# Three of a pair's four weight sums in DRAM, in two halves, and the fourth on VectorE

## The chip, the cores and the metric

The kernel runs on one core of a Trainium2 chip. The metric is device time in microseconds for one execution of the whole program; the number compared is the median of several runs.

A core has five engines, each with its own instruction stream that it works through in order: TensorE (PE, matrix products), VectorE (DVE), ScalarE (ACT), GpSimd (POOL) and SyncE (SP, here only a queue that starts transfers). They are held together by semaphores. Transfers between DRAM and the on-chip memory are carried out by 16 DMA engines, which all queues share. GpSimd's queue can also start a copy that adds to its target ("accumulating copy").

## The reference, cut to what matters

One decoder layer on 256 tokens of width 1024: pooling and attention heads in parallel, an output projection and a layer norm, a cross-attention into 256 memory tokens and a layer norm, and then the part that this case is about:

```python
def swiglu(h, w_gate, w_up, w_down):
    return (jax.nn.silu(h @ w_gate) * (h @ w_up)) @ w_down

h = layer_norm(DEEPNORM_ALPHA * h + swiglu(h, w_gate[l], w_up[l], w_down[l]), ln3_g[l], ln3_b[l])
```

The inner width is 2816. All inputs and outputs are float32.

## The kernel before

**Two terms per number.** TensorE multiplies a reduced float32 (called F32R) at full speed. So each operand is split into `hi`, its value rounded to F32R, and `lo`, the rest; a product is made of three: hi·hi, hi·lo and lo·hi (`three`, lines 386 to 391). Splitting a weight tile of 128 x 1024 takes one cast on ScalarE (L171) and one subtraction on VectorE (L173).

**The stream of weights.** Class `Stream` holds all weight tiles in the order of use: w0, w1, and so on. `fetch` starts the load of a tile on SP's queue into one of seven raw buffers, `prepare` splits it, and `fetch_ahead` starts as many loads as there are raw buffers that no unsplit tile holds. Split tiles lie in eight pairs of buffers (nine from the third gate/up chunk on). Each engine's order is the order in which the program writes its instructions; no scheduler moves them. A load hook (`ws.before`) puts other transfers into SP's order ahead of a given tile.

**Gate and up.** The inner width is cut into 11 chunks of 256 columns. Chunk c uses four weight tiles; chunk 1 begins with w63 and chunk 10 ends with w102. Its four PSUM banks are read out by ScalarE (L990) and VectorE (L991, four adds of 128 x 256), and these instructions stand in the engines' order behind the splits of the tiles of the following chunk. Two sets of four banks alternate, so that chunk c + 2, or the first products of the last stage, wait until the banks of chunk c are read out. What comes out of a chunk is multiplied, split (L456, L457) and kept as `gT`.

**Down.** The last projection runs over the same 11 chunks. Chunks 1 to 8 are multiplied by a scheme with seven products in place of eight for two-by-two blocks: a chunk's 256 rows and the two halves of the columns make four quarters of weights, each 128 x 512. Besides the quarters the scheme needs sums of them. For chunks 7 and 8 VectorE makes those sums from the loaded quarters (`prepare_pair`, lines 123 to 147; three tiles of numbers for each chunk, w124 to w129). For chunks 1 to 6 (`SUMMED`) the sums are made in DRAM before the tiles are loaded. The host has put the quarters of these chunks in order in `w_sum`, four planes of [128, 6, 512]; the program makes two arrays of [128, 2, 6, 512]:

- `sum_z` begins as a copy of planes 1 and 2, and gets planes 2 and 3 added: (plane 1 + plane 2, plane 2 + plane 3).
- `sum_w` begins as a copy of planes 0 and 1; both its halves get the second sum of `sum_z` added, and its first half plane 1 as well.

The two plain copies of 3 MB each are started by SP (L353, L354), ahead of tiles w62 and w63. The four accumulating copies are in `add_quarters` (L356 to L363, issued by L358) on POOL's queue: one of 3 MB and three of 1.5 MB. POOL reaches them after the second layer norm's last small instruction.

Per chunk the stream then loads tile `y` (planes 0 and 1), `z` and `w`, and for every second chunk `o` (plane 3 of two chunks), each 128 x 1024. In the order of the stream they are y, o, z, w and y, z, w: w103 to w123. `summed` (L1080) multiplies them; each tile takes two products of three, on accumulators m[0] to m[7], which fill the eight banks. Chunks 0, 9 and 10 (w130 to w135) are multiplied plainly by `pieces`, and the layer norm ends the program.

Of the kernel before, what the change touches and what calls it, by code (L numbers as in the profile page):

```python
# [8 lines left out]
F32 = mybir.dt.float32  # L9
F32R = mybir.dt.float32r  # L10
AF = mybir.ActivationFunctionType
OP = mybir.AluOpType
AX = mybir.AxisListType

P = 128
# [24 lines left out]
SUMMED = (1, 2, 3, 4, 5, 6)  # L40
# [6 lines left out]
def r32(t):  # L47
    return t.bitcast(F32)


class Stream:
# [2 lines left out]

    def __init__(self, nc, raw_pool, pool):
        self.nc, self.raw_pool, self.pool = nc, raw_pool, pool
        self.pairs, self.corner = {}, {}
        self.src, self.raws, self.tiles, self.homes = [], [], [], []
        self.loads, self.splits = {}, {}
        self.used, self.held = 0, True  # L60
        self.pace, self.asked = 1, 0
        self.cuts, self.casts = {}, {}
        self.late, self.ahead = None, W_BUFS
# [8 lines left out]
    def add_pair(self, upper, lower):  # L72

        first = len(self.src)
        self.src += [upper, lower, None]
        for i in range(3):
            self.pairs[first + i] = (first, i)
        return range(first, first + 3)  # L80

    def before(self, number, load):

        self.loads.setdefault(number, []).append(load)
# [5 lines left out]
    def fetch(self, upto, queue):  # L90

        while len(self.raws) < min(upto, len(self.src)):
            i = len(self.raws)
            for load in self.loads.pop(i, []):
                load()
            src = self.src[i]
            if i < len(self.homes):
                raw = self.homes[i]
            else:
                raw = self.raw_pool.tile(self.shape(i), F32, tag="raw", name=f"w{i}r")  # L100
            if src is not None:
                for s, q in self.cuts.get(i, [(slice(None), queue)]):
                    q.dma_start(raw[:, :, s], src[:, :, s])
            self.raws.append(raw)

    def shape(self, i):
        return list((self.src[i - 1] if self.src[i] is None else self.src[i]).shape)

    def widen(self, pool):
# [3 lines left out]
    def fetch_ahead(self):  # L113

        while len(self.raws) < len(self.src):
            i, done = len(self.raws), len(self.tiles)
            waiting = [j for j in range(len(self.homes), i)
                       if (self.pairs[j][0] + 2 if j in self.pairs else j) >= done]
            if len(waiting) >= RAW_BUFS:
                break  # L120
            self.fetch(i + 1, self.nc.sync)
# [27 lines left out]
    def prepare(self, upto, eng=None):  # L149
        nc = self.nc  # L150
        while len(self.tiles) < min(upto, len(self.src)):
            i = len(self.tiles)
            src = self.src[i]
            for split in self.splits.pop(i, []):
                split()
            self.fetch(i + 1, nc.sync)
            raw = self.raws[i]
            shape = self.shape(i)
            pool = self.pool
            if self.late and (i - self.late[0]) % self.ahead < LATE_BUFS:  # L160
                pool = self.late[1]
            hi = pool.tile(shape, F32R, tag="hi", name=f"w{i}h")
            lo = pool.tile(shape, F32R, tag="lo", name=f"w{i}l")
            if i in self.pairs:
                self.prepare_pair(i, hi, lo)
                self.tiles.append((hi, lo))
                self.fetch_ahead()
                continue
            for group in self.casts.get(i, [[slice(None)]]):
                for s in group:  # L170
                    nc.scalar.copy(hi[:, :, s], raw[:, :, s])  # L171
                s = slice(group[0].start, group[-1].stop)
                (eng or nc.vector).tensor_sub(lo[:, :, s], raw[:, :, s], r32(hi[:, :, s]))  # L173
            self.tiles.append((hi, lo))
            self.fetch_ahead()
# [32 lines left out]
def decoder_layer(  # L208
# [3 lines left out]
    nc = tc.nc  # L212
# [14 lines left out]
    def bank(name):  # L227
        return pb.tile([P, 512], F32, tag="b", name=name)
# [5 lines left out]
    ws = Stream(nc, rp, wp)  # L234
# [5 lines left out]
    def rows(w, k0, c0, nk=1, width=D):  # L240
        return ws.add(w[k0 * P:(k0 + nk) * P, c0:c0 + width].rearrange("(k p) n -> p k n", p=P), 1)

    def block(w, at, shape):

        j, n = shape
        return w[at:at + P * j * n].rearrange("(p j n) -> p j n", p=P, j=j)

    c_qk = []
    for k in range(KD):
        if k < 3:  # L250
            first = [ws.add(block(w_qkv, (2 * k + j) * P * 512, (1, 512)), 1)[0] for j in range(2)]
# [6 lines left out]
    c_u = [cols(w_u, c) for c in range(2)]  # L258
    c_xk = [cols(w_xk, c) for c in range(4)]
    c_mix = [rows(w_out, k, 0) for k in range(KD)]  # L260
    for numbers in c_mix[:5]:
        ws.cuts[numbers[0]] = [(slice(0, 512), nc.sync), (slice(512, D), nc.sync)]
    c_xv = [rows(w_xkv, k, D) for k in range(KD)]
    c_xq = [cols(w_xq, c) for c in range(4)]
    c_xo = [rows(w_xo, k, 0) for k in range(KD)]
    c_gu = [ws.add(w_gu[c], 4) for c in range(NFC)]
    dram = ctx.enter_context(tc.tile_pool(name="dram", bufs=1, space=bass.MemoryType.DRAM))
    sum_z, sum_w = [dram.tile([P, 2, len(SUMMED), 512], F32, name=f"sum_{name}") for name in "zw"]
    c_dn = {}
    for c in DOWN:  # L270
        tiles = [w_down[k * P:(k + 1) * P, :].rearrange("(k p) n -> p k n", p=P) for k in (2 * c, 2 * c + 1)]
        if c in SUMMED:
            j = SUMMED.index(c)
            order = [("y", w_sum[:, 0:2, j, :]), ("z", sum_z[:, :, j, :]), ("w", sum_w[:, :, j, :])]
            if j % 2 == 0:
                order.insert(1, ("o", w_sum[:, 3, j:j + 2, :]))
            c_dn[c] = {what: ws.add(src, 1)[0] for what, src in order}
        elif c in SEVEN:
            c_dn[c] = ws.add_pair(*tiles)
        else:  # L280
            c_dn[c] = [ws.add(w, 1)[0] for w in tiles]
# [68 lines left out]
    ws.before(c_dn[LAST[0]][1], load_norm("b", 3, ln3_b))  # L350


    ws.before(c_gu[0][3], lambda: nc.sync.dma_start(sum_z, w_sum[:, 1:3]))  # L353
    ws.before(c_gu[1][0], lambda: nc.sync.dma_start(sum_w, w_sum[:, 0:2]))  # L354

    def add_quarters():  # L356
        def add(dst, src):
            nc.gpsimd.dma_start(dst, src, accum_op=OP.add, max_dma_last_dim=8192)  # L358

        add(sum_z, w_sum[:, 2:4])  # L360
        for i in range(2):
            add(sum_w[:, i], sum_z[:, 1])
        add(sum_w[:, 0], w_sum[:, 1])  # L363

    ident = cp.tile([P, P], F32, name="ident")
    make_identity(nc, ident)
# [29 lines left out]
    def proj_both(pss, numbers, yT, group=KD):  # L396

        for k0 in range(0, KD, group):  # L400
            for k in range(k0, k0 + group):
                hi, _ = ws.get(numbers, k)
                for b, ps in enumerate(pss):
                    nc.tensor.matmul(ps, hi[:, b * P:(b + 1) * P], yT.both(k), start=k == 0, stop=False,  # L404
                                     skip_group_check=True)
                yield
            for k in range(k0, k0 + group):
                _, lo = ws.parts_of(numbers, k)
                for b, ps in enumerate(pss):
                    nc.tensor.matmul(ps[:, S:], lo[:, b * P:(b + 1) * P], yT.pair(k)[0], start=False,  # L410
                                     stop=k == KD - 1, skip_group_check=True)
                ws.done(numbers, k)
                if ws.pace == 1:
                    ws.next()
                yield
# [31 lines left out]
    def run(gen, n=None):  # L447

        while n is None or n > 0:
            if next(gen, gen) is gen:  # L450
                return False
            n = None if n is None else n - 1
        return True
# [559 lines left out]
    first = [bank("pg") for t in range(T)]  # L1013
# [10 lines left out]
    for c in range(1, NFC):  # L1024
        pss = [(accbank if c % 2 else bank)("pg") for _ in range(4)]
        if c == 3:
            ws.widen(late)
            add_quarters()
        gu = proj_both(pss, c_gu[c], h2T, KD if c < NFC - 3 else 2)
        run(gu, 2)  # L1030
        if left:
            left.multiply()
        run(gu, 2)
        if left:
            left.split()
        else:
            run(gu, 4)
            gated_t()
        if c == NFC - 1:
            run(gu, 7)  # L1040
            ws.held = True
        run(gu)
        left = Gated(c, pss)
        left.add()
# [200 lines left out]
```

## Time and profile before

| | us |
|---|---|
| median of 3 runs | 378.41 (377.07 to 378.56) |
| profiled execution, whole | 378.57 |
| its span, first to last instruction | 376.8 |
| PE busy in the span | 368.5 |
| DVE busy | 298.2 |
| ACT busy | 206.6 |
| POOL busy | 24.5 |

The profile is one execution, seen by the hardware profiler. The granted TensorE clock was 0.999 of full speed. Of 90.80 MB moved, 82.13 MB went through SP's queue and 7.86 MB through POOL's, which is that of the accumulating copies; the latter took 10.3% of the 16 DMA engines' time.

In a row of the chain stand start, length, engine, tile and line. A row of a timeline has start and length in us, engine, line, operation, output and inputs with their shapes, a count, and in brackets how long the engine stood idle before it and what released it. The length of an instruction on VectorE or ScalarE reaches a little into the next one, so starts are compared where instructions follow each other. In a list of transfers, the last number is the time from issue to landing. In a list of waits stand the total, the count and the longest. The last stage (down) begins at 314.98 us of the span.

### The profile page before, as it was taken

What the parts mean: (1) busy time and instruction counts of PE and PEld (TensorE: products, weight loads), DVE (VectorE), ACT (ScalarE), POOL (GpSimd) and SP (SyncE); (2) the same over time, 40 slices, a digit from 0 to 9 for tenths busy, and PEclk for the clock granted to TensorE, in tenths of its full rate; (3) what the DMA queues carried; (4) which work ended last, traced back from release to release, by engine and by line L of the source; (5) the groups of instructions that cost most, each with busy time, mean ns of one, the idle gap of its engine ahead of it and who ended that gap; (6) DMA issues with size and microseconds to landing.
All of it is one profiled execution on the core that took longest, in us unless ns stands there. A gap on an engine that the chain in (4) does not pass through costs nothing.

```text
span 376.8 us, 5614 instructions
## 1 busy us (share of the span) xinstructions
PE 368.5 (98%) x2058; PEld 317.2 (84%) x2058; DVE 298.2 (79%) x481; ACT 206.6 (55%) x330; POOL 24.5 (6%) x31
## 2 busy tenths in 40 slices
PE   9999999999999999999999999989999999999994
PEld 8997878787888889988888888868888888888882
DVE  6768799965699677865887468688888889989994
ACT  5746677644164636644145446465567668865510
POOL 1000033400010000000120101010000000000021
PEclk9999999999999999999999999999999999999999
DMA  7997674668509965998149999999655668996302
GB/s 268 414 416 270 217 286 139 198 221 285 165 0 301 374 214 181 348 334 315 57 79 232 340 272 355 291 318 335 236 192 172 199 195 255 300 401 260 94 0 111
DMA packets 26715, 90.80 MB, mean 241 GB/s; under 512 B 2624, under 2 KB 3392, under 8 KB 25920
## 3 DMA queue, kind: packets, MB, share of 16 engines
q1 hardware_dynamic: 25040, 82.13, 61.8%
q0 software_dynamic: 1216, 7.86, 10.3%
q10 hardware_dynamic: 432, 0.46, 0.3%
q8 instruction: 16, 0.26, 0.3%
q14 instruction: 11, 0.09, 0.1%
HBM read 89.39 MB, written 15.20 MB: 278 GB/s over the span
## 4 chain that ended last, share of the span: by engine, by line
PE 96%; DVE 1%; DMA 1%; ACT 1%; issue 0%; POOLq 0%; ACTq 0%
PE pg L404 20%; PE pg L410 10%; PE pqk L510 6%; PE m L389 5%; PE m L391 5%; PE m L390 5%; PE acc L389 4%; PE acc L390 4%; PE acc L391 4%; PE pxk L404 4%; PE pxq L404 4%; PE pxq L410 2%; PE pu L404 2%; PE pxk L410 2%; PE xv L389 2%; PE xv L391 2%
## 5 line engine op out<-in xcount | busy, mean ns | idle before, releaser
L456 ACT CAST g<-sg 128x512 fp32r<-128x512 f32 x16 | 9.9, 620 | 20.7 <-DVE sg L1010 14.8
L752 POOL TENSOR_TENSOR rs<-rs,mhalf 128x1 f32<-128x1 f32 x6 | 5.0, 832 | 238.5 <-DVE rs L751 238.5
L457 DVE TENSOR_TENSOR g<-sg,g 128x512 fp32r<-128x512 f32 x16 | 11.1, 692 | 9.6 <-ACT g L456 9.6
L991 DVE TENSOR_TENSOR sg<-pg,sg 128x256 f32<-128x256 f32 x40 | 14.1, 416 | 0.0
L990 ACT COPY sg<-pg 128x256 f32<-128x256 f32 x40 | 11.8, 378 | 0.6 <-PE pg L410 0.6
L995 ACT ACTIVATE sg<-sg 128x512 f32<-128x512 f32 x10 | 6.4, 635 | 10.0 <-DVE sg L991 10.0
L547 ACT ACTIVATE xpr<-xs,mx 128x256 f32<-128x256 f32 x8 | 3.7, 469 | 14.3 <-DVE mx L558 14.3
L547 ACT ACTIVATE pr<-pr,mx 128x128 f32<-128x128 f32 (+1 forms) x16 | 7.1, 445 | 7.6 <-DVE mx L578 7.6
L456 ACT CAST h2T<-tp 128x512 fp32r<-128x512 f32 x4 | 2.3, 586 | 13.0 <-PE tp L467 12.9
L757 DVE SCALAR_TENSOR_TENSOR r<-r,mv,gb 128x512 f32<-128x512 f32 (+2 forms) x12 | 8.2, 722 | 0.0
L744 DVE BATCH_NORM_STATS2 st<-r 128x6 f32<-128x512 f32 (+1 forms) x12 | 8.0, 670 | 0.3
L623 POOL TENSOR_TENSOR win<-upad 128x542 f32<-128x542 f32 x2 | 4.0, 1998 | 57.0 <-DVE upad L654 57.0
L996 DVE TENSOR_TENSOR sg<-sg 128x512 f32<-128x512 f32 x10 | 6.9, 691 | 0.8
L552 DVE RECIPROCAL sm<-sm 128x2 f32<-128x2 f32 x12 | 2.0, 166 | 6.0 <-ACT xpr L547 4.5
L862 PE MATMUL xs<-xkTh,xq 128*128 128x256 f32 x32 | 6.4, 282 | 0.0
L456 ACT CAST h1T<-tp 128x512 fp32r<-128x512 f32 x4 | 2.4, 588 | 7.1 <-PE tp L467 7.1
L762 DVE SCALAR_TENSOR_TENSOR h<-r,rs,gb 128x512 f32<-128x512 f32 x8 | 5.7, 747 | 0.1
L623 POOL TENSOR_TENSOR win<-win 128x269 f32<-128x269 f32 (+3 forms) x4 | 5.8, 1445 | 0.2
L662 ACT CAST xkTh<-pxk 128x256 fp32r<-128x256 f32 x8 | 2.6, 377 | 5.5 <-PE pxk L410 5.5
L664 DVE TENSOR_TENSOR xkl<-pxk,xkTh 128x256 f32<-128x256 f32 x8 | 3.0, 416 | 3.1 <-ACT xkTh L662 3.1
L862 PEld LDWEIGHTS xs<-xkTh,xq 128*128 128x128 f32 x32 | 5.2, 190 | 0.2
L171 ACT CAST w39h<-w39r 128x1024 fp32r<-128x1024 f32 x1 | 1.0, 1049 | 7.8 <-PE acc L391 7.8
(1132 smaller groups left out, 1286.4 us busy)
## 6 DMA issues: line engine op xcount, KB each, us to landing
sum_z<-in_w_sum SPq DMA_DIRECT2D x1, 3072.0 KB, 13.5
sum_w<-in_w_sum SPq DMA_DIRECT2D x1, 3072.0 KB, 18.8
sum_z<-in_w_sum POOLq DMA_DIRECT2D x1, 3072.0 KB, 21.1
sum_w<-sum_z POOLq DMA_DIRECT2D x2, 1536.0 KB, 15.6
gb<-in_ln_g SPq DMA_DIRECT2D x3, 512.0 KB, 6.2
gb<-in_ln_b SPq DMA_DIRECT2D x3, 512.0 KB, 9.2
sum_w<-in_w_sum POOLq DMA_DIRECT2D x1, 1536.0 KB, 14.6
wr<-in_w_qkv SPq DMA_DIRECT2D x5, 256.0 KB, 4.4
```

The source lines that it names most:

```text
L389: nc.tensor.matmul(ps, wa, ya, start=start, stop=False, skip_group_check=part)
L390: nc.tensor.matmul(ps, wa, yb, start=False, stop=False, skip_group_check=part)
L391: nc.tensor.matmul(ps, wb, ya, start=False, stop=stop, skip_group_check=part)
L404: nc.tensor.matmul(ps, hi[:, b * P:(b + 1) * P], yT.both(k), start=k == 0, stop=False, skip_group_check=True)
L410: nc.tensor.matmul(ps[:, S:], lo[:, b * P:(b + 1) * P], yT.pair(k)[0], start=False, stop=k == KD - 1, skip_group_check=True)
L456: nc.scalar.copy(h, ps)
L457: nc.vector.tensor_sub(l, ps, r32(h))
L510: nc.tensor.matmul(qk[i][:, f, :], w[:, c * P:(c + 1) * P], y, start=k == 0 and f == 0 and w is hi and y is x_hi, stop=k == KD - 1 and w i ...
L547: nc.scalar.activation(dst[:, j, :], src[:, j, :], AF.Exp, bias=mx[:, j:j + 1], scale=sign, accum_out=sm[:, j:j + 1])
L862: nc.tensor.matmul(ps[:, t, :], q[:, kk, t * P:(t + 1) * P], k[:, 2 * h + kk], start=n == 0, stop=q is q_lo and kk == 1, skip_group_check= ...
L990: nc.scalar.copy(y[:, f, :], ps[:, S:])
L991: nc.vector.tensor_add(y[:, f, :], ps[:, :S], y[:, f, :])
```

## The change

Tile w is made in two steps. Its second half (the sum of planes 1, 2 and 3) is still made in DRAM: `sum_w` now is [128, 6, 512], a copy of plane 1 to which the second sum of `sum_z` is added. The load brings this half only, 128 x 512, into the second half of the raw tile. The first half is made on chip: VectorE adds the first half of the chunk's raw tile y to it (L183 of the changed kernel), into the first half of the raw tile; then the tile is split like any other. The raw buffer of y is therefore held until that add (`held_raw`).

The order within a chunk becomes y, o, w, z and y, w, z; w is w105, w108, w112, w115, w119 and w122. In VectorE's order the add stands directly ahead of the subtraction of its tile, and ScalarE's cast of the tile reads what the add writes.

The copies in DRAM are made in two halves of three chunks each: on SP's queue 1.5 MB for `sum_z` ahead of w63 and 0.75 MB for `sum_w` ahead of w65, then the same for the second half ahead of w67 and w69. On POOL's queue there are again four accumulating copies: 1.5 MB, 0.75 MB, 1.5 MB, 0.75 MB; each pair's second reads what the first wrote.

Of the eight row blocks of `w_out` (w27 to w34), the first three instead of the first five are loaded in two halves of the columns.

```diff
+    def add_fourth(self, src, of):
+
+        number = len(self.src)
+        self.src.append(src)
+        self.fourth[number] = of
+        self.held_raw[of] = number
+        return number
...
-            if src is not None:
+            if i in self.fourth:
+                queue.dma_start(raw[:, 1:2, :], src)
+            elif src is not None:
...
             waiting = [j for j in range(len(self.homes), i)
-                       if (self.pairs[j][0] + 2 if j in self.pairs else j) >= done]
+                       if self.held_raw.get(j, j) >= done]
...
+            if i in self.fourth:
+                nc.vector.tensor_add(raw[:, 0], self.raws[self.fourth[i]][:, 0], raw[:, 1])
             for group in self.casts.get(i, [[slice(None)]]):
...
-    for numbers in c_mix[:5]:
+    for numbers in c_mix[:3]:
...
-    sum_z, sum_w = [dram.tile([P, 2, len(SUMMED), 512], F32, name=f"sum_{name}") for name in "zw"]
+    sum_z = dram.tile([P, 2, len(SUMMED), 512], F32, name="sum_z")
+    sum_w = dram.tile([P, len(SUMMED), 512], F32, name="sum_w")
...
-            order = [("y", w_sum[:, 0:2, j, :]), ("z", sum_z[:, :, j, :]), ("w", sum_w[:, :, j, :])]
+            c_dn[c] = {"y": ws.add(w_sum[:, 0:2, j, :], 1)[0]}
             if j % 2 == 0:
-                order.insert(1, ("o", w_sum[:, 3, j:j + 2, :]))
-            c_dn[c] = {what: ws.add(src, 1)[0] for what, src in order}
+                c_dn[c]["o"] = ws.add(w_sum[:, 3, j:j + 2, :], 1)[0]
+            c_dn[c]["w"] = ws.add_fourth(sum_w[:, j:j + 1, :], c_dn[c]["y"])
+            c_dn[c]["z"] = ws.add(sum_z[:, :, j, :], 1)[0]
...
-    ws.before(c_gu[0][3], lambda: nc.sync.dma_start(sum_z, w_sum[:, 1:3]))
-    ws.before(c_gu[1][0], lambda: nc.sync.dma_start(sum_w, w_sum[:, 0:2]))
-
-    def add_quarters():
-        def add(dst, src):
-            nc.gpsimd.dma_start(dst, src, accum_op=OP.add, max_dma_last_dim=8192)
-
-        add(sum_z, w_sum[:, 2:4])
-        for i in range(2):
-            add(sum_w[:, i], sum_z[:, 1])
-        add(sum_w[:, 0], w_sum[:, 1])
+    HALF = len(SUMMED) // 2
+
+    def begin_sums(i):
+        js = slice(i * HALF, (i + 1) * HALF)
+        nc.sync.dma_start(sum_z[:, :, js], w_sum[:, 1:3, js])
+
+    def begin_second(i):
+        js = slice(i * HALF, (i + 1) * HALF)
+        nc.sync.dma_start(sum_w[:, js], w_sum[:, 1, js])
+
+    for i in range(2):
+        ws.before(c_gu[i + 1][0], lambda i=i: begin_sums(i))
+        ws.before(c_gu[i + 1][2], lambda i=i: begin_second(i))
+
+    def add_quarters(i):
+        js = slice(i * HALF, (i + 1) * HALF)
+        nc.gpsimd.dma_start(sum_z[:, :, js], w_sum[:, 2:4, js], accum_op=OP.add, max_dma_last_dim=8192)
+        nc.gpsimd.dma_start(sum_w[:, js], sum_z[:, 1, js], accum_op=OP.add, max_dma_last_dim=8192)
...
-            add_quarters()
+            for i in range(2):
+                add_quarters(i)
```

More of the change, by code (lines that the diff above doesn't have):

```diff
@@ L56, in __init__ @@
         self.nc, self.raw_pool, self.pool = nc, raw_pool, pool
-        self.pairs, self.corner = {}, {}
+        self.pairs, self.corner, self.fourth, self.held_raw = {}, {}, {}, {}
         self.src, self.raws, self.tiles, self.homes = [], [], [], []
@@ L79, in add_pair @@
             self.pairs[first + i] = (first, i)
+            self.held_raw[first + i] = first + 2
         return range(first, first + 3)
+    def add_fourth(self, src, of):
[4 more added lines that the diff above has]
+        return number
     def before(self, number, load):
@@ L106, in shape @@
     def shape(self, i):
+        if i in self.fourth:
+            i = self.fourth[i]
         return list((self.src[i - 1] if self.src[i] is None else self.src[i]).shape)
@@ L168, in prepare @@
                 continue
+            if i in self.fourth:
+                nc.vector.tensor_add(raw[:, 0], self.raws[self.fourth[i]][:, 0], raw[:, 1])
             for group in self.casts.get(i, [[slice(None)]]):
```

## The prediction

> **What bounds the kernel now.** I read the page's first part, the chain and PE's waits, then the stretches and each engine's timeline. All rows are of one profiled execution: its span is 376.8 us, its own time 378.57 us, 0.16 us above the median of the three runs (378.41 us), so 1.77 us lie outside the span and are left alone.
>
> ```profile
> PE 368.5 (98%) x2058; PEld 317.2 (84%) x2058; DVE 298.2 (79%) x481; ACT 206.6 (55%) x330; POOL 24.5 (6%) x31
> PE pg L404 <- DVE sg L991: 1.9, 1, 1.9
> 223.50 7.28 PE pg L404 x32
> ...
> 234.61 7.28 PE pg L404 x32
> ...
> 245.89 1.23 DVE w83l L173
> 247.11 0.34 DVE sg L991
> 247.59 7.81 PE pg L404 x32
> ...
> 259.24 7.28 PE pg L404 x32
> ```
>
> TensorE is the bound. Inside the work it stops once: a gate/up chunk takes 234.61 to 247.59 = 12.98 us and the next one 11.65 us, where the undisturbed one from 223.50 took 11.11 us. The hole so costs 1.87 + 0.54 = **2.4 us**. What it waited for stands on VectorE, ScalarE and GpSimd:
>
> ```profile
> 191.51 1.44 POOL L358 DMA_DIRECT2D sum_z<-in_w_sum  x1
> 244.78 1.15 POOL L358 DMA_DIRECT2D sum_w<-in_w_sum  x1 [14.79 <-issue]
> sum_z<-in_w_sum POOLq DMA_DIRECT2D x1, 3072.0 KB, 21.1
> sum_w<-sum_z POOLq DMA_DIRECT2D x2, 1536.0 KB, 15.6
> sum_w<-in_w_sum POOLq DMA_DIRECT2D x1, 1536.0 KB, 14.6
> 243.55 1.05 ACT L171 CAST w82h<-w82r 128x1024 fp32r<-128x1024 f32 x1 [2.26 <-DMA w82r<-in_w_gu]
> 244.64 1.23 DVE L173 TENSOR_TENSOR w82l<-w82r,w82h 128x1024 fp32r<-128x1024 f32 x1 [1.90 <-ACT w82h L171]
> 210.31 1.22 DVE L173 TENSOR_TENSOR w70l<-w70r,w70h 128x1024 fp32r<-128x1024 f32 x1 [5.02 <-ACT w70h L171]
> 219.63 1.23 DVE L173 TENSOR_TENSOR w74l<-w74r,w74h 128x1024 fp32r<-128x1024 f32 x1 [1.57 <-ACT w74h L171]
> 229.61 1.23 DVE L173 TENSOR_TENSOR w76l<-w76r,w76h 128x1024 fp32r<-128x1024 f32 x1 [1.46 <-ACT w76h L171]
> w71r<-in_w_gu SPq DMA_DIRECT2D x1, 512.0 KB, 13.8
> w76r<-in_w_gu SPq DMA_DIRECT2D x1, 512.0 KB, 23.4
> ```
>
> From 191.5 to 259.4 us four accumulating copies run one after another, and weight loads land late beside them. The load of w82 makes VectorE late, and the evacuation of an earlier chunk's banks (L991) stands behind it in VectorE's order. The same starvation costs VectorE 5.02 + 1.57 + 1.46 + 1.90 = 9.95 us by then; it is still catching up at the end of the stage. The last stage (from 314.98) has no such hole, but VectorE is full:
>
> ```profile
> 315.00:330.00 15.00, 15.00 (x67) 12.40 (x67) 15.00 (x18) 12.59 (x17) 0.00 (x0) 1.00 0.89 275
> 314.98 0.23 PE m L389
> 315.51 1.41 DVE L991 TENSOR_TENSOR sg<-pg,sg 128x256 f32<-128x256 f32 x4
> 347.90 1.23 DVE L147 TENSOR_TENSOR w129l<-w127r,w129h 128x1024 fp32r<-128x1024 f32 x1
> 351.79 0.39 PE L390 MATMUL m<-w129l,g 128*128 128x512 f32 x1
> ```
>
> (Columns of a stretch: length, then PE, PEld, DVE, ACT, POOL busy.) VectorE needs all of 15 us, and w129l, done at 349.13, is read at 351.79: the smallest lead of the late tiles, **2.66 us**.
>
> **The change, part by part.**
>
> *Less traffic.* The accumulates shrink from 3 + 1.5 + 1.5 + 1.5 to 1.5 + 0.75 + 1.5 + 0.75 MB, the plain copies from 6 to 4.5 MB. POOL issues four as before, in order, each pair's second waiting for its first; they still start at 191.5. The first takes 10.5 us (half of 21.1) to 15.6; I take 10.5, since like the old one it starts before this stage's loads. The 1.5 MB one later takes 15.6, a 0.75 MB one 7.8 (half) to 15.6 at most; I take half. With 1.15 us an issue they end near 191.5 + 41.7 + 3.5 = 236.7, not 259.4. In one 15.6 us accumulate six tiles landed (w71 to w76, issued at 199.31 and 204.99, landed 13.8 and 23.4 us later), 2.6 us a tile. From w70 near the first one's end, 203, that puts w82 at 203 + 12 x 2.6 = 234, not 243.5. Without VectorE's 1.90 us for w82 alone L991 comes 1.9 us sooner, just what PE waits there; with the earlier waits shrunk too the hole closes with several us to spare. **-2.4 us** (nothing, at the other end).
>
> [...]
>
> *SP's queue.* It gets four copies instead of two, before w63, w65, w67 and w69 instead of w62 and w63.
>
> ```profile
> 179.92 0.33 SPq L103 DMA_DIRECT2D w69r<-in_w_gu  x1
> 195.84 1.05 ACT L171 CAST w63h<-w63r 128x1024 fp32r<-128x1024 f32 x1
> ```
>
> The last copy so goes out near 180, at a quarter of the size of the old ones, and no tile behind a copy is cast before 195.84. Two w_out rows are loaded whole instead of in halves: two issues of 0.33 us fewer, and PE's list of waits names no load. Both at nothing: the cover is the seven raw buffers; without it, a late load costs its lateness.
>
> *The fourth sum.* Six times, for w105, w108, w112, w115, w119 and w122, VectorE adds 128x512, then ScalarE casts, then VectorE subtracts. VectorE's order has nothing between add and subtraction, so it stands still while ScalarE casts. The pairs of the last chunks show that step:
>
> ```profile
> 339.33 0.68 DVE L143 TENSOR_TENSOR w124r<-w125r,w124r 128x512 f32<-128x512 f32 x1
> 339.93 1.22 DVE L144 TENSOR_TENSOR w125l<-w126r,w125h 128x1024 fp32r<-128x1024 f32 x1
> 340.12 1.05 ACT L146 CAST w126h<-w124r 128x1024 fp32r<-128x1024 f32 x1 [1.67 <-DVE w124r L143]
> 341.21 1.23 DVE L147 TENSOR_TENSOR w126l<-w124r,w126h 128x1024 fp32r<-128x1024 f32 x1
> ```
>
> From add to subtraction 341.21 - 339.33 = **1.88 us**; with the wait filled, as there by L144, an add costs 0.60. So 0.60 to 1.88 each; I take 1.88, as nothing fills it here. Behind the waiting subtraction stand all later splits and L991, and PE waits for those.
>
> The first two (w105, w108) lie before the last evacuation, which cannot start before PE is done at 314.98. VectorE reached it at 315.51, with no slack, so they would cost 2 x 1.88 less two small idles, 3.2 us, if VectorE came as now. It comes earlier: of the 9.95 us of starvation 2.4 + 3.2 = 5.6 must vanish for them to be hidden. Loads some 9 us earlier at w82 give that; **0** (3.2 at the other end).
>
> The other four cost 4 x 1.88 = 7.52 us of VectorE. Against that its waits for loads in this stage go, as it becomes slower than the loads:
>
> ```profile
> 329.46 1.22 DVE L173 TENSOR_TENSOR w120l<-w120r,w120h 128x1024 fp32r<-128x1024 f32 x1
> 331.47 1.22 DVE L173 TENSOR_TENSOR w121l<-w121r,w121h 128x1024 fp32r<-128x1024 f32 x1 [0.79 <-ACT w121h L171]
> 334.15 1.23 DVE L173 TENSOR_TENSOR w123l<-w123r,w123h 128x1024 fp32r<-128x1024 f32 x1
> 335.29 0.69 DVE L136 TENSOR_TENSOR w126r<-w124r 128x512 f32<-128x512 f32 x1
> 336.38 0.69 DVE L137 TENSOR_TENSOR w126r<-w125r,w124r 128x512 f32<-128x512 f32 x1 [0.40 <-DMA w125r<-in_w_down]
> 365.37 0.69 DVE L1136 TENSOR_TENSOR r<-m,r 128x512 f32<-128x512 f32 x1 [0.24 <-PE m L391]
> 367.52 0.42 DVE L1136 TENSOR_TENSOR r<-m,r 128x256 f32<-128x256 f32 x1 [0.73 <-PE m L391]
> 369.90 0.43 DVE L744 BATCH_NORM_STATS2 st<-acc 128x6 f32<-128x256 f32 x1 [1.49 <-PE acc L391]
> ```
>
> A split follows a split after 1.14 us. 0.87 us are lost before w121l, 0.40 from there to w123l, 0.49 before L137: 1.76 us. VectorE is 7.52 - 1.76 = 5.76 us late at w129l, the lead is 2.66, so PE is **+3.1 us** late. Behind that VectorE is 2.66 us late against PE, and the tail's idles hold 0.24 + 0.73 + 1.49 = 2.46: **+0.2**.
>
> *Raw buffers and smaller loads.* y's buffer is held until w's add, so one or two of seven loads start later; half-size w loads land sooner. Loads in that stage take 4 to 8 us and seven splits now take over 10: nothing, and a late load would cost VectorE its lateness. TensorE's products are the same 2058 in another order.
>
> Sum: 378.57 - 2.4 + 3.1 + 0.2 = **379.5 us**, +0.2%; against the median 0.16 less, within what I can claim.
>
> **Rivals.**
>
> *The lead isn't won* (20%). The loads come just early enough to close the hole, but the first two sums also stand on VectorE's path: + 3.2, 382.7 us. For it: a first accumulate of 15.6 us and small ones near 15.6 would keep the loads late to about 245. Against it: six tiles landed beside one.
>
> *The hole stays* (8%). Loads late as now, or another one on the edge: 382.7 + 2.4 = 385.1 us.
>
> *VectorE keeps up* (12%), the other side. If the add costs its 0.60 alone, because the casting engine is not waited for, the four cost 2.4 us, less 1.76, well inside 2.66: PE isn't delayed, and 378.57 - 2.4 = 376.2 us. It decides below (2.66 + 1.76) / 4 = 1.1 us a sum. Against it: that order has no other work to fill the wait.
>
> *A slowed TensorE clock* (3%). In the stretch of the hole the granted clock stayed 1.00, though the chunk behind it took 0.54 us too long. If PE's 3.1 us came as one wait and the clock then fell to half for as long, the loss would be 1.7 us more, 381.2 us; I expect waits of at most about 1 us each, spread over w119 to w129. [...]
>
> ```profile
> 244.80:250.00 5.20, 3.32 (x17) 2.52 (x16) 4.39 (x8) 3.39 (x7) 1.14 (x1) 1.00 1.06 369
> ```
>
> **How the numbers follow.** The likeliest case (52%) gives 379.5, its own range 378.5 to 381.0 (0.2 of the hole left, waits 0.1 to 0.3 us longer). 5% stay for what I don't see. Half a per cent, 1.9 us, is about what a measurement tells from no change: 376.5 to 380.3 is the same. The likeliest puts 0.40 there and 0.12 above; the lost lead, the staying hole and the slow clock add 0.31 above; keeping up gives 0.11 below. With the rest: faster 0.11, same 0.45, slower 0.44. From 377.4 to 383.0 the range leaves out the hole that stays and keeping up, 2 in 10.
>
> **What would show it.** PE's wait for L991 is gone and chunks keep 11.1 us; the last accumulate is issued near 228, not 244.78. Add to subtraction is 1.9 us on each of six w tiles. PE gets short waits for splits between w119 and w129, about 3 us. Wrong if loads still land 13 us or more after 230, if L991 of the last chunk starts well behind PE's end, or if PE has no waits in the last stage.

## The result, and the profile after

The changed kernel takes 380.37 us (median of 6 runs, 379.94 to 381.24) against 378.22 us before (6 runs, 377.07 to 378.56): a ratio of 1.0064, 95% interval 1.0047 to 1.0081. It is slower by about 2 us; 379.5 was forecast, with a range of 377.4 to 383.0.

The profiled execution took 380.30 us, with a span of 378.5 us and a granted clock of 0.999; the one of before 378.57 and 376.8. The rows below are to be compared with the rows of before in the prediction. First the page's busy times and PE's list of waits (total, count, longest) of the changed kernel:

```profile
PE 370.2 (98%) x2058; PEld 317.5 (84%) x2058; DVE 301.2 (80%) x487; ACT 206.2 (54%) x330; POOL 23.5 (6%) x31
PE m L414 <- DVE w127l L153: 0.8, 1, 0.8
PE m L414 <- DVE w124l L153: 0.8, 1, 0.8
PE m L414 <- DVE w127c L151: 0.2, 1, 0.2
```

The 1.9 us wait for the evacuation of the banks is gone. In its place stand waits for splits of the last chunks' tiles, and none of a whole microsecond. The chain of the changed kernel shows the gate/up chunks at an even pace:

```profile
235.13 7.28 PE pg L428 x32
...
246.25 7.28 PE pg L428 x32
...
257.36 7.28 PE pg L428 x32
```

Each takes 11.1 us, the one that took 12.98 before and its successor (11.65) too. The hole is closed: 2.4 us won. The accumulating copies are shorter and the weight loads beside them land sooner (that this is what closes the hole is tested below, in e3, e5 and e8). POOL's timeline and the list of transfers (KB of each, us from issue to landing) of the changed kernel:

```profile
192.07 1.20 POOL L386 DMA_DIRECT2D sum_z<-in_w_sum  x1
203.73 0.84 POOL L387 DMA_DIRECT2D sum_w<-sum_z  x1 [10.46 <-DMA sum_z<-in_w_sum]
204.26 1.41 POOL L386 DMA_DIRECT2D sum_z<-in_w_sum  x1
224.96 0.84 POOL L387 DMA_DIRECT2D sum_w<-sum_z  x1 [19.29 <-DMA sum_z<-in_w_sum]
sum_z<-in_w_sum POOLq DMA_DIRECT2D x2, 1536.0 KB, 15.9
sum_w<-sum_z POOLq DMA_DIRECT2D x2, 768.0 KB, 10.0
w76r<-in_w_gu SPq DMA_DIRECT2D x1, 512.0 KB, 17.8
w82r<-in_w_gu SPq DMA_DIRECT2D x1, 512.0 KB, 11.7
```

The last one is issued at 224.96, not at 244.78, and w76 lands after 17.8 us instead of 23.4. VectorE's waits for late loads have shrunk to these three:

```profile
214.91 1.22 DVE L188 TENSOR_TENSOR w74l<-w74r,w74h 128x1024 fp32r<-128x1024 f32 x1 [0.73 <-ACT w74h L186]
224.49 1.23 DVE L188 TENSOR_TENSOR w76l<-w76r,w76h 128x1024 fp32r<-128x1024 f32 x1 [1.06 <-ACT w76h L186]
226.29 1.23 DVE L188 TENSOR_TENSOR w77l<-w77r,w77h 128x1024 fp32r<-128x1024 f32 x1 [0.57 <-ACT w77h L186]
```

0.73 + 1.06 + 0.57 = 2.36 us, against 12.06 before: the prediction's 9.95, and 2.11 us ahead of w71 that it leaves out. The sums then take this back. VectorE's timeline of the changed kernel around the last evacuation (L1015, the third row) and at one of the last four sums:

```profile
299.79 0.68 DVE L183 TENSOR_TENSOR w105r<-w103r,w105r 128x512 f32<-128x512 f32 x1
301.72 1.23 DVE L188 TENSOR_TENSOR w105l<-w105r,w105h 128x1024 fp32r<-128x1024 f32 x1 [1.25 <-ACT w105h L186]
313.25 1.42 DVE L1015 TENSOR_TENSOR sg<-pg,sg 128x256 f32<-128x256 f32 x4 [1.19 <-ACT sg L1014]
323.84 0.69 DVE L183 TENSOR_TENSOR w115r<-w114r,w115r 128x512 f32<-128x512 f32 x1
325.77 1.23 DVE L188 TENSOR_TENSOR w115l<-w115r,w115h 128x1024 fp32r<-128x1024 f32 x1 [1.25 <-ACT w115h L186]
```

From add to subtraction it takes 1.93 us, of which VectorE stands still for 1.25 while ScalarE casts. The first two sums are still covered: after them VectorE has to wait 1.19 us for the last banks. The other four are not. PE's timeline and the tail's statistics on VectorE, changed kernel:

```profile
343.55 0.50 PE L414 MATMUL m<-w124l,g 128*128 128x512 f32 x1 [0.77 <-DVE w124l L153]
350.24 0.50 PE L414 MATMUL m<-w127l,g 128*128 128x512 f32 x1 [0.78 <-DVE w127l L153]
312.94 0.40 PE L413 MATMUL m<-w103h,g 128*128 128x512 f32 x1
371.59 0.43 DVE L768 BATCH_NORM_STATS2 st<-acc 128x6 f32<-128x256 f32 x1 [0.32 <-PE acc L415]
```

From the first product of the last stage to these statistics it takes 371.59 - 312.94 = 58.65 us. Before it was 369.90 - 314.82 = 55.08 us, by the same two instructions:

```profile
314.82 0.40 PE L389 MATMUL m<-w103h,g 128*128 128x512 f32 x1
```

So the stage is 3.57 us longer. The list of waits shows only 1.8 of it, since it counts pauses alone and leaves out the shortest. Where the rest lies can be seen from w128 and w129, whose subtractions and first products are these, two rows of before and three of the changed kernel:

```profile
346.62 1.22 DVE L144 TENSOR_TENSOR w128l<-w129r,w128h 128x1024 fp32r<-128x1024 f32 x1
350.43 0.39 PE L390 MATMUL m<-w128l,g 128*128 128x512 f32 x1
```

```profile
350.70 1.22 DVE L157 TENSOR_TENSOR w128l<-w129r,w128h 128x1024 fp32r<-128x1024 f32 x1
351.98 0.50 PE L414 MATMUL m<-w128l,g 128*128 128x512 f32 x1
353.46 0.40 PE L414 MATMUL m<-w129l,g 128*128 128x512 f32 x1
```

The product with w129l begins 353.46 - 312.94 = 40.52 us into the stage; before it was 351.79 - 314.82 = 36.97. All but 0.02 us of the loss has come by then.

Together: 3.57 - 2.4 = +1.2 us. The two spans differ by 1.7, because the profiled execution of the changed kernel also lost 0.5 us at its start. Its first four products took 1.22 us, those of before 0.82:

```profile
3.77 1.22 PE L534 MATMUL pqk<-xT,w0h 128*128 128x256 f32 x4
```

```profile
3.84 0.82 PE L510 MATMUL pqk<-xT,w0h 128*128 128x256 f32 x4
```

All work up to the hole is late by that (chunk 1 begins at 201.39 instead of 200.86). Nothing ties it to the change: in the profiles of the experiments the same row is 0.82 twice and 1.20 to 1.22 six times, also in a kernel that is the one of before but for its copies, and over all ten profiles chunk 1 begins between 200.86 and 201.50. What makes these products slow in some executions is not shown: the granted clock reads 1.00 over these rows in both profiles, and each kernel was profiled once.

### The profile page after: what moved, and what is told of

It reads as the page before. It is cut to its first block, busy times and chain, and to the rows that moved or that the text cites. A ratio compares the mean times of both kernels' runs of the same rounds, so it can differ in the third digit from the quotient of the medians.

```text
span 378.5 us, 5619 instructions
## 1 busy us (share of the span) xinstructions
PE 370.2 (98%) x2058; PEld 317.5 (84%) x2058; DVE 301.2 (80%) x487; ACT 206.2 (54%) x330; POOL 23.5 (6%) x31
## 4 chain that ended last, share of the span: by engine, by line
PE 87%; DVE 7%; ACT 2%; issue 2%; POOLq 0%; ACTq 0%; DVEq 0%
PE pg L428 19%; PE pg L434 10%; PE pqk L534 6%; PE acc L413 4%; PE acc L414 4%; PE acc L415 4%; PE pxq L428 4%; PE pxk L428 4%; PE pxq L434 2%; PE pu L428 2%; PE pxk L434 2%; PE xv L413 2%; PE xv L415 2%; PE xv L414 2%; PE m L414 2%
## 5 line engine op out<-in xcount | busy, mean ns | idle before, releaser
L481 DVE TENSOR_TENSOR g<-sg,g 128x512 fp32r<-128x512 f32 x16 | 11.1, 691 | 9.6 <-ACT g L480 9.6
L1015 DVE TENSOR_TENSOR sg<-pg,sg 128x256 f32<-128x256 f32 x40 | 14.1, 414 | 1.2 <-ACT sg L1014 1.2
L1019 ACT ACTIVATE sg<-sg 128x512 f32<-128x512 f32 x10 | 6.4, 635 | 10.5 <-DVE sg L1015 10.5
L480 ACT CAST h2T<-tp 128x512 fp32r<-128x512 f32 x4 | 2.3, 586 | 13.0 <-PE tp L491 12.9
```

Source lines behind the costliest of these rows:

```text
L480: nc.scalar.copy(h, ps)
L481: nc.vector.tensor_sub(l, ps, r32(h))
L1015: nc.vector.tensor_add(y[:, f, :], ps[:, :S], y[:, f, :])
```

## The experiments

All are compared with the kernel before on the same chip. The last column is the last stage, from its first product to the last statistics, in the profiled execution.

| run | edit | median us | ratio to before (95%) | last stage us |
|---|---|---|---|---|
| before | | 378.2 to 378.4 | 1 | 55.08 |
| changed kernel | | 380.37 | 1.0064 (1.0047 to 1.0081) | 58.65 |
| e1_early_add | add ahead of the previous subtraction | 376.37 | 0.9953 (0.9940 to 0.9965) | 55.08 |
| e2_no_add | no add on VectorE | 376.59 | 0.9957 (0.9945 to 0.9970) | 55.08 |
| e3_old_traffic | before's copies, the new sums | 385.27 | 1.0189 (1.0175 to 1.0203) | 61.79 |
| e4_cuts5 | five cut rows as before | 380.29 | 1.0062 (1.0048 to 1.0075) | 58.70 |
| e5_whole | copies not in halves | 383.32 | 1.0135 (1.0109 to 1.0161) | 61.85 |
| e6_double_add | each add twice | 383.58 | 1.0139 (1.0113 to 1.0166) | 61.60 |
| e7_first_two_early | e1 for w105 and w108 alone | 380.28 | 1.0055 (1.0037 to 1.0074) | 58.69 |
| e8_before_halves | before with its copies in halves | 379.65 | 1.0039 (1.0023 to 1.0054) | 55.08 |

### The wait inside the sum

In e1 the add of the next tile goes ahead of this tile's subtraction, so that VectorE has this subtraction to do while ScalarE casts:

```diff
-            if i in self.fourth:
-                nc.vector.tensor_add(raw[:, 0], self.raws[self.fourth[i]][:, 0], raw[:, 1])
...
+                if i + 1 in self.fourth:
+                    self.fetch(i + 2, nc.sync)
+                    nxt = self.raws[i + 1]
+                    nc.vector.tensor_add(nxt[:, 0], self.raws[self.fourth[i + 1]][:, 0], nxt[:, 1])
                 (eng or nc.vector).tensor_sub(lo[:, :, s], raw[:, :, s], r32(hi[:, :, s]))
```

> The changed kernel with one thing moved: VectorE's add for a w tile stands ahead of the subtraction of the tile before it, so that ScalarE casts w while VectorE still has that subtraction to do. Same adds, same transfers. My theory (the cost of the change is VectorE standing still while ScalarE casts): add to the subtraction of w no longer 1.88 us but about 0.60 plus up to 0.2 of waiting, four of them 3.2 us less 1.8 us of old load waits, inside VectorE's lead of 2.66; TensorE's waits and slow restarts in the last stage (3.55 us in the profile) go, the time is 380.4 - 3.5 = 376.9 us, 376.2 to 377.4, faster than the kernel before by about 0.4%. Rival (the adds themselves, six more VectorE instructions, are too much for that engine): 380 us as now. Rival (the late y buffers or the w loads hold VectorE): 379 to 380 us.

Measured: 376.37 us (376.08 to 376.55). VectorE's timeline of e1:

```profile
313.03 1.42 DVE L1017 TENSOR_TENSOR sg<-pg,sg 128x256 f32<-128x256 f32 x4 [3.32 <-ACT sg L1016]
321.15 0.68 DVE L189 TENSOR_TENSOR w115r<-w114r,w115r 128x512 f32<-128x512 f32 x1
321.76 1.22 DVE L190 TENSOR_TENSOR w114l<-w114r,w114h 128x1024 fp32r<-128x1024 f32 x1
323.09 1.23 DVE L190 TENSOR_TENSOR w115l<-w115r,w115h 128x1024 fp32r<-128x1024 f32 x1
367.81 0.43 DVE L770 BATCH_NORM_STATS2 st<-acc 128x6 f32<-128x256 f32 x1 [1.48 <-PE acc L417]
```

From add to subtraction it is still 1.94 us, but the subtraction of w114 fills it. VectorE waits 3.32 us instead of 1.19 for the last banks, PE's list of waits names none in the last stage, the stage takes 55.08 us as before the change, and the tail waits for PE again (1.48). This version is faster than both kernels.

In e2 the add is left out, and the load of w brings the DRAM sum into both halves of the tile, with twice the bytes:

```diff
-                queue.dma_start(raw[:, 1:2, :], src)
+                queue.dma_start(raw, src.to_broadcast(self.shape(i)))
...
-            if i in self.fourth:
-                nc.vector.tensor_add(raw[:, 0], self.raws[self.fourth[i]][:, 0], raw[:, 1])
```

> The changed kernel without VectorE's adds: the load of a w tile brings the sum from DRAM into both halves (512 KB as before the change), so the first half holds a wrong sum, and nothing is added on chip. Traffic in DRAM, order of the tiles and hold of the y buffers as changed. My theory (less traffic is worth the 2.4 us hole, the add costs 3.5 us): no hole at the fifth chunk, no TensorE wait in the last stage, 380.4 - 3.5 = 376.9 us, 376.0 to 377.4. Rival (the order y, w, z and the held y buffers cost something themselves): 378 us or more.

Measured: 376.59 us (376.2 to 376.88), no waits of PE in the last stage. With the wait filled (e1) and without the add (e2) the time is the same but for 0.2 us. So six adds of 0.6 us fit into VectorE's lead, and what the sums cost is the wait that each add puts into VectorE's order. e2 has the new order of the tiles and holds the y buffers as the change does, so neither costs anything that shows.

### Only the last four cost

e7 issues the add early, as e1 does, for w105 and w108 alone. Against e1:

```diff
+            if i in list(self.fourth)[2:]:
+                nc.vector.tensor_add(raw[:, 0], self.raws[self.fourth[i]][:, 0], raw[:, 1])
...
-                if i + 1 in self.fourth:
+                if i + 1 in list(self.fourth)[:2]:
```

> The changed kernel, with the add issued ahead of the previous tile's subtraction (which fills the wait for ScalarE) for the first two sums, w105 and w108, alone; w112, w115, w119 and w122 stay as in the change. With all six that way the time was 376.37 us. Theory that the first two were hidden ahead of the last evacuation and the last four cost all: nothing gained, 380.3 us (379.8 to 380.8), the same waits in the last stage, and VectorE waits about 2.5 us longer for the last banks. Rival, that the first two are part of the price: 377.5 to 379.3 us.

Measured: 380.28 us (380.07 to 380.62), nothing gained. VectorE's wait for the last banks grows to 3.22 us, 2.0 more where about 2.5 were expected, and PE's waits in the last stage are the same as in the changed kernel:

```profile
313.06 1.42 DVE L1019 TENSOR_TENSOR sg<-pg,sg 128x256 f32<-128x256 f32 x4 [3.22 <-ACT sg L1018]
```

### A dose

e6 issues each add of the changed kernel twice:

```diff
             if i in self.fourth:
                 nc.vector.tensor_add(raw[:, 0], self.raws[self.fourth[i]][:, 0], raw[:, 1])
+                nc.vector.tensor_add(raw[:, 0], self.raws[self.fourth[i]][:, 0], raw[:, 1])
```

> The changed kernel with each of the six adds issued twice in a row (the second writes the same values again). A dose of 0.60 us of VectorE's time for each sum, in the place where the wait stands. Theory that PE's 3.3 to 3.5 us in the last stage are VectorE's lateness: the last four add 4 x 0.60 = 2.4 us there, the first two 1.2 us, which the 1.19 us that VectorE waits for the last evacuation's banks covers: 382.7 us (382.2 to 383.3), PE waits for splits from w119 to w129 2.4 us more. Rival, that loads or the order of the tiles make these waits and VectorE has room: 380.3 us (to 381).

Measured: 383.58 us (382.72 to 384.11), 3.2 us more than the changed kernel where 2.4 were expected; the last stage grew by 61.60 - 58.65 = 2.95. The size was off: the second add doesn't start 0.60 us after the first but 0.72, in VectorE's timeline of e6:

```profile
317.62 0.68 DVE L183 TENSOR_TENSOR w112r<-w110r,w112r 128x512 f32<-128x512 f32 x1
318.34 0.69 DVE L184 TENSOR_TENSOR w112r<-w110r,w112r 128x512 f32<-128x512 f32 x1
320.28 1.23 DVE L189 TENSOR_TENSOR w112l<-w112r,w112h 128x1024 fp32r<-128x1024 f32 x1 [1.25 <-ACT w112h L187]
```

4 x 0.72 = 2.9 us, the growth of the stage (2.95). What VectorE loses there, PE loses, nearly one to one.

### The fewer bytes, and the halves

e3 keeps the new sums and the new order of the tiles, with the copies of before:

```diff
-    sum_w = dram.tile([P, len(SUMMED), 512], F32, name="sum_w")
+    sum_z, sum_w = [dram.tile([P, 2, len(SUMMED), 512], F32, name=f"sum_{name}") for name in "zw"]
...
+        add(sum_z, w_sum[:, 2:4])
+        for i in range(2):
+            add(sum_w[:, i], sum_z[:, 1])
+        add(sum_w[:, 0], w_sum[:, 1])
```

> The kernel before with VectorE's fourth sum and the changed order of tiles alone: plain and accumulating copies in DRAM of the old sizes, at the old places (the accumulates for w's first half are still made, and not used). My theory (the first two sums of six are hidden only because the loads come early; and the hole is there because the accumulates are long): the hole of 2.4 us stays, the lost lead costs 3.2 us more than the changed kernel, 380.4 + 2.4 + 3.2 = 386.0 us less up to 1 us that the start took longer in the profile of the changed kernel, so 384.5 to 386.0. Rival (all six sums cost what they cost anywhere, traffic is worth only the hole): 382.8 us. Rival (traffic doesn't matter): 380.4 us.

Measured: 385.27 us (385.15 to 385.48), as expected. PE's waits in e3:

```profile
PE m L405 <- DVE sg L1007: 1.4, 1, 1.4
PE pg L420 <- DVE sg L1007: 1.2, 1, 1.2
```

The hole stays (second row), and VectorE comes late to the last evacuation (first row), so the first two sums cost too: the last stage takes 61.79 us, 3.1 more than in the changed kernel.

e5 has the new, smaller sums with the copies in one piece, 3 and 1.5 MB:

```diff
-    HALF = len(SUMMED) // 2
+    HALF = len(SUMMED)
...
-    for i in range(2):
+    for i in range(1):
...
-            for i in range(2):
+            for i in range(1):
                 add_quarters(i)
```

> The changed kernel, with the copies and accumulating copies in DRAM in one piece instead of two halves: plain copies of 3 and 1.5 MB ahead of w63 and w65, then accumulating copies of 3 and 1.5 MB. The bytes (4.5 MB accumulated instead of 7.5) are the same as in the changed kernel. Theory that the hole closed because of the fewer bytes: they end near 230 us, no wait of PE for the evacuation (L1015) comes back, 380.3 us (379.8 to 380.9, the changed kernel's own time). Rival, that the two halves are what closed it (their parts overlap, small ones hold the engines less long): PE waits for an evacuation again by up to 1.9 us, 381.5 to 382.8 us.

Measured: 383.32 us (382.74 to 384.21), beyond what either side gave. My expectation fell, and the rival was right only that the halves matter, not where. Of the hole little comes back (one chunk of 11.54 us where the others take 11.1), but the lead isn't won: PE's wait, VectorE's last evacuation, ScalarE's casts and POOL's second copy in e5:

```profile
PE m L413 <- DVE sg L1015: 1.5, 1, 1.5
317.44 1.41 DVE L1015 TENSOR_TENSOR sg<-pg,sg 128x256 f32<-128x256 f32 x4
209.66 1.05 ACT L186 CAST w70h<-w70r 128x1024 fp32r<-128x1024 f32 x1 [6.16 <-DMA w70r<-in_w_gu]
214.06 1.05 ACT L186 CAST w71h<-w71r 128x1024 fp32r<-128x1024 f32 x1 [2.86 <-DMA w71r<-in_w_gu]
214.00 1.16 POOL L387 DMA_DIRECT2D sum_w<-sum_z  x1 [20.44 <-DMA sum_z<-in_w_sum]
```

The first accumulating copy of 3 MB runs until about 213.6, and w70 and w71, needed from 204 on, land only near its end. SP's plain copies had ended by then: the second took 12.9 us and stands ahead of the load of w67, issued at 172.69, so it had landed by 185.6 us. So it is the accumulating one that they wait beside. In the changed kernel the first one is done by 203.7, and w70 is cast at 204.61:

```profile
204.61 1.05 ACT L186 CAST w70h<-w70r 128x1024 fp32r<-128x1024 f32 x1 [1.22 <-DMA w70r<-in_w_gu]
```

So the last evacuation starts at 317.44 in e5 and at 313.25 in the changed kernel. The same bytes in one piece cost 3.0 us by the medians, most of it in the last stage (61.85 us, 3.2 more in the profiled executions); about 0.5 us lies where the hole was.

e8 is the kernel before with its copies cut into halves, all four sums in DRAM (`begin_z` and `begin_w` are the plain copies of a half):

```diff
+    halves = [slice(0, 3), slice(3, 6)]
+    for i, js in enumerate(halves):
+        ws.before(c_gu[i + 1][0], lambda js=js: begin_z(js))
+        ws.before(c_gu[i + 1][2], lambda js=js: begin_w(js))
...
+        for js in halves:
+            add(sum_z[:, :, js], w_sum[:, 2:4, js])
+            for i in range(2):
+                add(sum_w[:, i, js], sum_z[:, 1, js])
+            add(sum_w[:, 0, js], w_sum[:, 1, js])
```

> The kernel before with one part of the change alone: its copies and accumulating copies in two halves of three chunks (copies ahead of w63, w65, w67 and w69, then 1.5, 0.75, 0.75, 0.75 MB accumulated, and the same again); all four sums in DRAM, the same 7.5 MB accumulated. Theory that the bytes make the loads late: the hole stays, 377.7 to 379.0 us, with PE's wait for the evacuation of 1 us or more. Rival, that halves alone close it, because the second half's first copy runs beside the first half's last: 375.5 to 376.6 us, which would be the price of the change without its sums.

Measured: 379.65 us (379.31 to 381.21), slower than before, and outside what both sides gave. In its profiled execution (381.21 us, the longest of its runs) the hole has only moved:

```profile
PE pg L413 <- DVE sg L1000: 2.1, 1, 2.1
231.89 1.23 DVE L173 TENSOR_TENSOR w77l<-w77r,w77h 128x1024 fp32r<-128x1024 f32 x1 [4.27 <-ACT w77h L171]
```

VectorE now waits 4.27 us for w77 and comes late to the evacuation of an earlier chunk. Halves without fewer bytes don't close the hole; fewer bytes without halves do but for about 0.5 us, and don't cover the first two sums. The gain of the change needs both.

### The cut rows

e4 is the changed kernel with five rows of `w_out` loaded in halves, as before:

```diff
-    for numbers in c_mix[:3]:
+    for numbers in c_mix[:5]:
```

> The changed kernel with five w_out rows loaded in halves again, as before the change. My theory: nothing, 380.4 us within 0.4. Rival (the two whole loads cost or save something in the first stages): a difference of over 0.5 us, seen as TensorE being earlier or later at the first products with w_out.

Measured: 380.29 us (380.23 to 380.88). The three rows instead of five make no difference.

## Why the prediction was right, and where its sizes were off

The sum came out 0.9 us short of the median, with the right terms. As a change it is less than half: 0.93 us were added to the profiled execution of before, and the medians differ by 2.15. The two profiled executions differ by 1.73 = 0.93 + 0.27 of the last stage + 0.53 at the start; a further 0.35 us is that the profiled execution of before was the longest of its six, and 0.07 that the one of the changed kernel lies below its median. Point by point:

- *Less traffic closes the hole, -2.4 us.* Right: the wait is gone, every chunk takes 11.1 us. The way to it was only half right. POOL's four copies were taken one after another, ending at 236.7; the third was issued 0.5 us after the second and ran beside it, for 204.26 to 224.96 = 20.7 us instead of 15.6. That the errors cancel is luck: the last is issued at 224.96 and, with the 10.0 us of such a copy, ends near 235; w82 landed at 223.46 + 11.7 = 235.2, forecast 234.
- *The first two sums are hidden, 0.* Right, and tested by e7: moving their adds gains nothing. VectorE had 1.19 us to spare where they end. The prediction put this down to loads that come earlier; e5 shows that it hangs on the size of the pieces, and w70 and w71 point at the first one. With the same bytes in one piece the lead isn't won, and the rival of that name (+3.2, 382.7 us) is what comes out: 383.32 us.
- *The last four sums, +3.1, and the tail, +0.2.* The step was right, e1 and e2 show that the wait inside each sum is what costs. Its size was 3.57 instead of 3.3: 3.55 at w129l and 0.02 behind it, so the tail's +0.2 did not come. VectorE was (350.70 - 312.94) - (346.62 - 314.82) = 5.96 us late instead of 5.76, since a sum took 1.92 to 1.93 us instead of 1.88. The smallest lead was not w129l's 2.66 us, as the prediction read it, but w128l's: done at 347.84, read at 350.43, 2.59. That makes 5.96 - 2.59 = 3.37, and the last 0.2 us is that PE's first products behind a pause took longer (0.50 us instead of 0.39, at 343.55, 350.24 and 351.98).
- *The cuts and SP's queue, 0.* Right for the cuts (e4). SP's copies weren't tried alone.
- *The start.* The prediction took the start to be the same in both executions. It was 0.5 us longer in the profile after. With 0.27 us of the last stage that gives 0.8 us between the forecast and the profiled execution of 380.30 us. The start need not be what makes the other runs as long, though: e4's profiled execution has the short one, its last statistics come 0.44 us sooner, ScalarE's last copy too (374.17 against 374.61), and its span is 378.5 us all the same, so it loses that behind the last computation. Half a microsecond between executions stays open.

The rivals became real kernels. Loads in time but no lead: forecast 382.7, e5 took 383.32. The hole stays and the lead isn't won: 385.1, e3 took 385.27. VectorE keeps up: 376.2, e1 took 376.37; the prediction's condition for it was an add that costs its 0.60 us alone, and its reason against it that "that order has no other work to fill the wait". Putting one instruction of other work there was enough. The slowed clock did not come in the changed kernel: its waits in the last stage were below 0.8 us, and the granted clock stayed at 1.00 there. (The rival's price was a little high: half of 3.1 us is 1.55, not 1.7. That a wait would halve the clock was the author's assumption; before, the clock stayed at 1.00 behind the wait of 1.9 us. Of the ten profiles e8's alone shows a fall in the middle of the work: 0.50 for about 3.4 us, behind a wait of 2.06.)

## What to carry to other kernels

In this kernel an add put into VectorE's order cost its own 0.68 us and the wait that it places there, 1.25 us. That wait for the other engine's answer decided between slower (380.37 us) and faster (e1, 376.37 us), and it was gone by issuing the add one instruction earlier; so look for what can stand between the two halves of a round trip before counting the round trip. And when background copies starve the loads, look at the size of each piece as well as at the bytes: w70 was cast at 204.61 us beside a first piece that ended at 203.7, and at 209.66 beside one that ran to 213.6.

## What the runs showed of the hardware

The TensorE clock did fall once in the middle of the work, after a shorter wait than the prediction feared. In the profiled execution of e8, PE waited 2.06 us, and from about 238.2 to 241.6 the granted clock was half. The rows are PE's timeline, and two stretches (length, busy time of PE, PEld, DVE, ACT and POOL, then the clock, the DMA share and GB/s; in the first the clock is a mean, as it falls inside):

```profile
237.11 3.42 PE L413 MATMUL pg<-h2T,w75h 128*128 128x512 f32 x8 [2.06 <-DVE sg L1000]
238.10:238.60 0.50, 0.50 (x2) 0.43 (x2) 0.50 (x1) 0.00 (x0) 0.00 (x0) 0.60 1.49 418
239.10:240.60 1.50, 1.50 (x5) 1.22 (x4) 0.82 (x3) 0.62 (x1) 0.00 (x0) 0.50 0.97 235
```

That part of the chunk took 9.48 us instead of 7.28, so the wait and what followed it cost 4.3 us. The kernel before waited 1.9 us at a like place, kept its clock at 1.00 and took 7.81, so about 1.7 us go with the slowed clock; e8's profiled execution is 1.6 us above its median, which fits an execution that had the fall where most had not. In the nine other profiles the clock is 1.00 from 238.2 to 241.6. That the wait brought the fall is argued from its place, about 1 us behind it, and not tested; how long a wait has to be for it is not shown.

An accumulating copy of 1.5 MB took 11.7 us from 192.07, mostly ahead of this stage's loads, and 20.7 us from 204.26, beside them and, at first, beside the 0.75 MB copy, in the same execution. The one of 3 MB took 21.1 us in the kernel before. So here the time of such a copy could not be halved with its bytes: 10.5 us were forecast for the first and 7.8 for those of 0.75 MB, which took 10.0. And two adds in a row that write the same 128 x 512 start 0.72 us apart; where the instruction behind the add writes another tile, as in e1 (321.15 to 321.76), it is 0.61.

In the profile of before a product of 128 x 256 takes TensorE 0.12 us with F32R operands (eight of L410, from 242.68 to 243.64) and 0.25 us with plain float32 ones, in two records (L634, from 62.15 to 62.40), at a granted clock of 1.00. That is all that the runs show of the "full speed" of F32R.
